# Eleven runs of products on zeros between the warm-up and the first real product

## The chip, the cores and the metric

One core of a Trainium2 chip runs the whole program. The metric is the device time of one execution in microseconds (us). Three runs of the kernel before took 2436.01, 2436.24 and 2447.96 us; the median is 2436.24.

## The reference

The reference runs a residual stream of 512 tokens by 1024 channels (float32) through two blocks. The first block has two layers. Each layer mixes a sliding-window attention, a short convolution and a diagonal complex recurrence (SSM) under gates, and then applies a gated feed-forward. The second block has a mixer with two kinds of sparse attention, a cross-attention to a memory of 256 rows, and a feed-forward with squared ReLU. Cut to what matters here, the beginning of the first layer:

```python
h = rmsnorm(x, norm_mix[i])
proj = h @ w_in[i]
q, k, v, cb, cc, cx, u, g = jnp.split(proj, IN_SPLITS, axis=-1)
...
lam_bar = jnp.exp(lam * dt)          # tables of the recurrence, from the inputs alone
_, states = lax.associative_scan(combine, (a_elems, bu), axis=1)
```

## The kernel before

Channels lie on the 128 partitions and the 512 tokens along the free axis. A value is kept as the sum of two float32r parts, high and low, and a product of weights and values is three float32r passes (lines 437 to 439): high by high, high by low, low by high. Weights come in 373 chunks of 128 by 1024 float32, each with eight 128 by 128 blocks. A chunk is loaded by SP's queue into one of three raw buffers, split by ScalarE (line 369, high part) and VectorE (line 370, low part) into one of three split buffers, and used by TensorE. Loads and splits are emitted with a raised priority.

The program is written as one sequence with side work (generators that are advanced between chunks). A scheduler then orders the instructions of each engine by priority, which is mostly program order, and by when its own model thinks that their inputs are ready; it also sets the waits. So an engine's order can differ from the program's: an instruction far down may come first where the engine would have nothing else to do.

The start goes so. SP loads a part of the vectors, the eight input tiles X, the first weight chunks and the constants (lines 1992 to 2001). GpSimd fills a bf16 tile `wz` with zeros (line 2008), and TensorE runs 16 warm-up products on it into one PSUM bank (line 2011), whose result is never read. Then the first norm splits each X[m] (lines 457 and 461) and adds up squares (lines 535 to 539, some of the additions on GpSimd). VectorE begins the tables of the recurrence (`_ssm_tables`, lines 818 to 1000), which need vectors only. `_gen_mix` computes the first result `u` of four tiles from 96 products in k-major order, with the norm's sums (line 492) and its broadcast (line 503) between the chunks, and evacuates it (line 579) with the row factor of the norm. After it come k, v and q.

PSUM has four banks for products under the tag `mm`, which go round; `u` holds all four. SBUF tiles under the same tag share their place: `wz` has the tag of the table `ssmc` (loaded at lines 960 and 961), and the tables `Wr` and `Wi` (lines 974 to 979) have the tags `wr` and `wi`. `Wr` and `Wi` have one column filled first (lines 976 and 977) and then copies and products written into them.

Of the kernel before, what the change touches and what calls it, by code (L numbers as in the profile page):

```python
# [11 lines left out]
FT = mybir.dt.float32  # L12
FR = mybir.dt.float32r
# [5 lines left out]
PSUM = bass.MemoryType.PSUM  # L19
DRAM = bass.MemoryType.DRAM  # L20
# [13 lines left out]
# ---------------------------------------------------------------- host layout  # L34
# [67 lines left out]
def _constants():  # L102
    """Arrays that depend on shapes alone."""
    f = np.float32
    lay = _cst_layout()
    c = np.zeros((128, lay["_n"][0]), f)

    def put(name, a):
        s, n = lay[name]
        c[:, s:s + n] = a  # L110
    put("ident", np.eye(128, dtype=f))
    q = np.arange(128)[:, None]
    j = np.arange(128)[None, :]
    put("mask1", np.concatenate([np.where(j > q, 0.0, NEG), np.where(j <= q, 0.0, NEG)], 1))
    t = np.arange(512).reshape(4, 128).T
    end = np.arange(32) * 16 + 31
    mc = np.where((end[None, None, :] <= t[:, :, None]) & (np.arange(32) < 31), 0.0, NEG)
    put("maskc", mc.reshape(128, 128))
    put("valid", (t >= 31).astype(f))
    put("stack", (np.arange(128)[:, None] % 32 == np.arange(128)[None, :] % 32).astype(f))  # L120
    put("ones2", 1.0)
    put("half2", (np.arange(128)[:, None] // 64 == np.arange(2)[None, :]).astype(f))
    rope = np.zeros((4, 128, 512), f)
    pos = np.arange(512, dtype=f)
    inv = (f(500000.0) ** (-np.arange(0, 16, 2, dtype=f) / f(16))).astype(f)
    ang = pos[:, None] * inv[None, :]
    cos, sin = np.cos(ang).T, np.sin(ang).T
    rope[0] = 1.0
    for h in (0, 64):
        rope[0, h:h + 8] = cos  # L130
        rope[0, h + 8:h + 16] = cos
        rope[1, h:h + 8] = -sin
        rope[1, h + 8:h + 16] = sin
    inv2 = (f(10000.0) ** (-np.arange(32, dtype=f) / f(32))).astype(f)
    ang = pos[:, None] * inv2[None, :]
    cos, sin = np.cos(ang).T, np.sin(ang).T
    C = np.concatenate([cos[:16], cos[:16], cos[16:], cos[16:]])
    S = np.concatenate([-sin[:16], sin[:16], -sin[16:], sin[16:]])
    rope[2] = np.concatenate([C, C])
    rope[3] = np.concatenate([S, S])  # L140
    cc = np.zeros((128, 256), f)
    n = end[:31]
    cc[:31, :128] = rope[2][:, n].T
    cc[:31, 128:] = rope[3][:, n].T
    put("crope", cc)
    return c, rope


def _host_pack(x, ins):
    """Layout only: transposes, permutations, repeats and zero padding."""  # L150
# [122 lines left out]
# ---------------------------------------------------------------- device  # L273
class _Net:
# [26 lines left out]
    # ---- memory  # L301
# [5 lines left out]
    def rslot(self):  # L307
        """A slot whose every writer rounds to float32r."""
        s = self.free_r.popleft()
        self.low_r = min(self.low_r, len(self.free_r))  # L310
        return s
# [30 lines left out]
    # ---- weights  # L342
# [8 lines left out]
    def _dma_(self):  # L351
        i = self.wd
        t = self.wp.tile([128, 1024], FT, tag="raw", bufs=self.RAW, name="raw")
        # the first chunk in halves: the products can start on its front
        n = 512 if i == 0 else 1024
        for c in range(0, 1024, n):
            self.nc.sync.dma_start(t[:, c:c + n], self.T["wp"][i, :, c:c + n])
        self.raw[i] = t
        self.wd += 1
# [34 lines left out]
    # ---- scheduling  # L394
# [19 lines left out]
    # ---- products  # L414
    def prod(self, key, K, ms, rhs, evac, outer=True, kk=None, N=512):
        """out[m] = sum_k W[k,m].T @ rhs[k] in three float32r passes; yields after each chunk."""
# [35 lines left out]
    # ---- pieces  # L452
    def split(self, src, g=None):
        """src * g as the exact sum of two float32r parts."""
        nc = self.nc
        h, l = self.rslot(), self.rslot()
        nc.scalar.activation(h, src, AF.Copy, scale=1.0 if g is None else g)  # L457
        if g is None:
            nc.vector.tensor_tensor(l, src, h.bitcast(FT), op=OP.subtract)  # L459
        else:  # L460
            nc.vector.scalar_tensor_tensor(l, src, g, h.bitcast(FT), op0=OP.mult, op1=OP.subtract)
        return (h, l)
# [10 lines left out]
    def rsqrt(self, out, ps, n, scale, eps, p=128):  # L473
        """out = 1/sqrt(ps * scale + eps) on a few columns."""
# [14 lines left out]
    def few(self, out, lhs, rhs, start=True, stop=True):  # L489
        """out = lhs.T @ rhs with few columns: the rows of out in four column tiles side by side."""  # L490
        for c in range(0, 128, 32):
            self.nc.tensor.matmul(out[c:c + 32], lhs[:, c:c + 32], rhs, start=start, stop=stop,
                                  skip_group_check=True)

    def tok_sums(self, ps, src, nblk=4):
        """ps(blk) = sums of src over partitions, tokens on partitions."""
        for b in range(nblk):
            self.few(ps(b), src[:, b * 128:(b + 1) * 128], self.ones1)

    def bcast(self, r, out, psum, nblk=4, width=None):  # L500
        """out[c, tok] = r[tok] for all c."""
# [5 lines left out]
    def heads_back(self, src, t, dst):  # L507
        """dst = two float32r parts of channel tile t of src[n], tokens on partitions."""
# [6 lines left out]
    def parts(self, o, dst, n):  # L515
        """Query block n of four channel tiles, from one bank, as two float32r parts."""
# [7 lines left out]
    def apply_v(self, out, pt, v, start, stop):  # L524
        """out[q, d] += sum_k pt[k, q] v[k, d]; the queries in two column tiles."""
# [3 lines left out]
    # ---- norms: raw split first, the row factor is applied to the product  # L529
# [12 lines left out]
    def norm_fin(self, st):  # L542
        """side steps that turn the sums into st['rs'], the row factor on all partitions."""
# [16 lines left out]
def _gen_mix(N, i, X, st, st2, tab=None):  # L560
    """First block's mixing half of layer i."""
# [10 lines left out]
    # --- SSM input  # L572
# [18 lines left out]
    # --- q, k, v  # L591
# [32 lines left out]
    # --- conv  # L624
# [26 lines left out]
    # --- gated branches  # L651
# [39 lines left out]
    # --- SSM tail: gelu, glu  # L691
# [36 lines left out]
def _gen_attn1(N, i, qT, kv, out):  # L728
# [13 lines left out]
    def probs(n, P):  # L742
        """Probabilities of the eight heads of query block n over its two key blocks."""
# [74 lines left out]
def _ssm_tables(N, i):  # L818
    """exp, cos, sin of the discretised poles, and what follows from them, on few columns."""
# [87 lines left out]
    # (lam_bar - 1) / lam  # L907
# [22 lines left out]
    # powers of lam_bar  # L930
# [8 lines left out]
    # b_bar  # L939
# [24 lines left out]
    # rotation per chunk of 8 and decay per chunk  # L964
# [17 lines left out]
    while n < 64:  # L982
        # W^n, then W^(n..2n-1)
# [18 lines left out]
def _gen_ssm(N, i, Ud, Yd, Kd, out):  # L1002
    """Diagonal complex recurrence, 64 chunks of 8 steps; four rounds of 128 channels (8 groups)."""
# [11 lines left out]
    for r in range(4):  # L1015
        pr = slice(4 * r, 4 * r + 4)
        # inputs with (step, channel) on partitions, steps from last to first
# [28 lines left out]
        # state contribution of each chunk  # L1046
# [22 lines left out]
        # back to the fixed frame, moved on by one chunk  # L1069
# [13 lines left out]
        # output side: C lam^t, t = 0..7  # L1083
# [8 lines left out]
        # kernels inside a chunk  # L1092
# [88 lines left out]
def _gen_att2(N, X, st, st2, gg, mem=None):  # L1181
    """Second block's mixer. X gets the residual sum, st2 the next norm's pieces."""
# [14 lines left out]
    # ---- row factors of the two norms  # L1197
# [17 lines left out]
    # x waits in DRAM while the slots are short  # L1215
# [5 lines left out]
    def residual():  # L1221
        """The normed x that the block adds to."""
# [17 lines left out]
    def rope(src, g=None):  # L1240
        """Rotated src * g; src may be in PSUM."""
# [22 lines left out]
    # ---- latents, index keys, gates: the row factor s1 is folded into later ones  # L1264
# [10 lines left out]
    def latents():  # L1275
# [33 lines left out]
        # index keys: gain and bias after the rows are turned back, both halves alike  # L1309
# [3 lines left out]
        # index weights take the queries' row factor, which is positive  # L1313
# [13 lines left out]
    # ---- heads with a norm: the row factor goes into the softmax's scale  # L1327
# [13 lines left out]
    def fold(out, src, n, div, row, rowq, mul):  # L1341
        """out = mul * row / sqrt(src * row^2 / div + eps); src (b, head), one row factor for each b."""
# [46 lines left out]
    def values():  # L1389
        """Both value heads of two branches with the tokens on partitions."""  # L1390
# [20 lines left out]
    def latent_kv():  # L1411
        """The shared key and value head, tokens on partitions."""
# [29 lines left out]
    # ---- compressed keys and values  # L1442
# [23 lines left out]
    def compress(z, ws):  # L1466
# [21 lines left out]
        if z == 1:  # L1488
            # the values of a query head's group, on the diagonal blocks of the four heads' keys
# [35 lines left out]
    # ---- index scores and the choice of keys  # L1525
# [42 lines left out]
    # ---- attention: units (n, branch, t) of two heads, queries of block n over all keys up to it  # L1568
# [74 lines left out]
    def compressed():  # L1643
        """The branch over the compressed keys; all heads of a block at once."""
        for n in range(4):
# [20 lines left out]
            # rows before the first whole block see no key  # L1666
# [32 lines left out]
    # ---- the order of things  # L1699
# [79 lines left out]
def _gen_memkv(N, M):  # L1779
    """Keys and values of the memory; yields between the pieces."""  # L1780
# [52 lines left out]
    # norm of the row-scaled keys: eps meets the scaled mean square  # L1833
# [28 lines left out]
def _gen_mem2(N, X, st, st2, M):  # L1862
# [3 lines left out]
    # ---- queries  # L1866
# [115 lines left out]
def tile_two_blocks(ctx: ExitStack, tc: tile.TileContext, T, out, nch, parts=None, dump=None):  # L1982
# [23 lines left out]
    # the tensor engine's clock is up when the first data arrive  # L2006
# [3 lines left out]
    for _ in range(16):  # L2010
        nc.tensor.matmul(ps, wz[:, :128], wz, start=True, stop=True)
    st = N.new_norm()
# [9 lines left out]
    # gains of the norm between the blocks and of the next norm, in one  # L2022
# [90 lines left out]
```

## Time and profile before

| | before |
|---|---|
| median of three runs | 2436.24 us |
| span of the profiled execution | 2433.1 us |
| TensorE busy | 2398.7 us |
| VectorE busy | 1440.4 us |
| ScalarE busy | 858.6 us |
| first warm-up product | 1.31 us |
| first real product | 7.00 us |

The page of the profile gives the profiled execution's time as its span, from the first instruction to the last; the median of the runs is 3.1 us above it. A busy time of TensorE counts a tail after each product, so two products in a row overlap; what a product costs in a stream is the step between two starts. The granted clock (PEclk) is a share of 2.4 GHz.

### The profile page before, as it was taken

The numbers are of one execution on the slowest core, as the hardware profiler recorded it, in microseconds if no ns is written. First come the engines' busy times: TensorE is split into PE (matmuls) and PEld (weight loads), VectorE is DVE, ScalarE is ACT, GpSimd is POOL, SyncE is SP. The second block draws the span as 40 slices with busy tenths as digits, with TensorE's granted clock in tenths as the row PEclk, the third lists the DMA queues.
The fourth block names the chain that finished last, engine by engine and source line by source line (L and its number), as shares of the span: only waits on it lengthen the run. The fifth ranks groups of instructions, "written<-read, shape, count | busy, mean of one in ns | idle before, by whom it ended". The sixth has DMA issues, their size and how long they took to land. (4 is left out here: it accounts for less than half of the span.)

```text
span 2433.1 us, 33742 instructions
## 1 busy us (share of the span) xinstructions
PE 2398.7 (99%) x13354; PEld 1880.1 (77%) x13357; DVE 1440.4 (59%) x2894; ACT 858.6 (35%) x1442; POOL 28.7 (1%) x48
## 2 busy tenths in 40 slices
PE   8999999999999999999999999999899999999999
PEld 6777888888888877778888888887666677888887
DVE  9976567543434677755554343467979766543443
ACT  3233333422222323433333222243456545422321
POOL 1000000000000000000000000000000000000000
PEclk9999999999999999999999999999979999999999
DMA  5322332222222233233222223242201111222222
GB/s 189 100 87 91 113 100 95 91 92 95 104 95 96 104 108 93 83 100 102 95 94 89 95 95 104 96 145 82 96 2 58 49 70 54 94 95 96 95 94 80
DMA packets 96781, 225.98 MB, mean 93 GB/s; under 512 B 35440, under 2 KB 39664, under 8 KB 96624
## 3 DMA queue, kind: packets, MB, share of 16 engines
q1 hardware_dynamic: 96624, 223.84, 27.1%
q8 instruction: 105, 1.72, 0.3%
q14 instruction: 52, 0.43, 0.1%
HBM read 214.88 MB, written 8.91 MB: 92 GB/s over the span
## 5 line engine op out<-in xcount | busy, mean ns | idle before, releaser
L437 PE MATMUL mm<-r,hi 128*128 128x512 f32 x2928 | 1163.7, 398 | 3.1 <-DVE f L579 2.2
L439 PE MATMUL mm<-r,lo 128*128 128x512 f32 x2928 | 1157.2, 395 | 4.5 <-DVE lo L370 4.5
L438 PE MATMUL mm<-r,hi 128*128 128x512 f32 x2928 | 1157.2, 395 | 0.0
L369 ACT ACTIVATE hi<-raw 128x1024 fp32r<-128x1024 f32 (+1 forms) x374 | 395.3, 1057 | 1240.3 <-PE mm L438 857.2
L437 PEld LDWEIGHTS mm<-r,hi 128*128 128x128 f32 x2928 | 551.3, 188 | 145.2 <-issue 4.2
L439 PEld LDWEIGHTS mm<-r,lo 128*128 128x128 f32 x2928 | 551.1, 188 | 135.8 <-DVE lo L370 4.9
L438 PEld LDWEIGHTS mm<-r,hi 128*128 128x128 f32 x2928 | 551.4, 188 | 127.7
L370 DVE TENSOR_TENSOR lo<-raw,hi 128x1024 fp32r<-128x1024 f32 (+1 forms) x374 | 456.1, 1220 | 222.1 <-ACT hi L369 220.6
L1152 DVE TENSOR_TENSOR f<-mm,f 128x512 f32<-128x512 f32 x88 | 60.9, 692 | 235.0 <-PE mm L439 235.0
L663 DVE TENSOR_TENSOR f<-mm,f 128x512 f32<-128x512 f32 x48 | 33.1, 689 | 103.1 <-PE mm L439 99.4
L457 ACT ACTIVATE r<-f 128x512 fp32r<-128x512 f32 x108 | 68.2, 632 | 60.5 <-DVE f L1158 29.2
L459 DVE TENSOR_TENSOR r<-f,r 128x512 fp32r<-128x512 f32 x108 | 74.0, 688 | 10.6 <-ACT r L457 7.4
L1174 DVE TENSOR_TENSOR f<-mm,f 128x512 f32<-128x512 f32 x48 | 33.1, 690 | 65.5 <-PE mm L439 65.3
L1959 DVE SCALAR_TENSOR_TENSOR f<-mm,f 128x512 f32<-128x512 f32 x32 | 22.1, 692 | 81.1 <-PE mm L439 81.1
L1974 DVE TENSOR_TENSOR f<-mm,f 128x512 f32<-128x512 f32 x32 | 22.1, 692 | 64.8 <-PE mm L439 64.7
L1580 PE MATMUL sc<-f,f 64*128 64x128 f32 (+3 forms) x192 | 53.5, 510 | 0.5 <-DVE f L1654 0.3
L1616 DVE TENSOR_REDUCE sm<-sc 128x1 f32<-128x128 f32 (+3 forms) x96 | 43.9, 483 | 16.1 <-PE sc L1582 15.8
L1590 PE MATMUL pt<-cst,f 128*128 128x128 f32 x240 | 43.9, 294 | 6.3 <-ACT f L1622 5.4
L527 PE MATMUL ot<-f,f 128*64 128x64 f32 x960 | 46.6, 235 | 0.0
L457 ACT ACTIVATE r<-f,vec 128x512 fp32r<-128x512 f32 x48 | 34.3, 714 | 32.5 <-DVE f L1174 7.8
L527 PEld LDWEIGHTS ot<-f,f 128*64 128x64 f32 x960 | 36.5, 142 | 11.7 <-issue 9.8
L1622 ACT ACTIVATE f<-sc,sm,rqn 128x128 f32<-128x128 f32 (+3 forms) x64 | 38.9, 613 | 15.3 <-DVE sm L1617 15.3
(387 smaller groups left out, 1741.7 us busy)
## 6 DMA issues: line engine op xcount, KB each, us to landing
raw<-in_wp_dram SPq DMA_DIRECT2D x372, 512.0 KB, 3.5
f<-in_xT_dram SPq DMA_DIRECT2D x8, 256.0 KB, 4.7
ud<-f SPq DMA_DIRECT2D x8, 256.0 KB, 2.3
f<-ud SPq DMA_DIRECT2D x64, 32.0 KB, 3.4
f<-ud SPq DMA_DIRECT2D x8, 256.0 KB, 3.6
yd<-f SPq DMA_DIRECT2D x64, 32.0 KB, 2.1
f<-yd SPq DMA_DIRECT2D x8, 256.0 KB, 3.6
xd<-f SPq DMA_DIRECT2D x8, 256.0 KB, 2.2
```

The source lines that it names most:

```text
L369: self.nc.scalar.activation(h[:, s], r[:, s], AF.Copy)
L370: self.nc.vector.tensor_tensor(lo[:, s], r[:, s], h.bitcast(FT)[:, s], op=OP.subtract)
L437: nc.tensor.matmul(p, wh, rh, start=first, stop=False)
L438: nc.tensor.matmul(p, wh, rl, start=False, stop=False)
L439: nc.tensor.matmul(p, wl, rh, start=False, stop=last)
L457: nc.scalar.activation(h, src, AF.Copy, scale=1.0 if g is None else g)
L459: nc.vector.tensor_tensor(l, src, h.bitcast(FT), op=OP.subtract)
L527: self.nc.tensor.matmul(out[c:c + 64], pt[:, c:c + 64], v, start=start, stop=stop, skip_group_check=True)
L1152: V.tensor_tensor(z, ps, RS, op=OP.mult)
L1580: PE.matmul(ps[h][:, :w], q[t][hs, n * 128:(n + 1) * 128], k_of[br][hs, :w], start=True, stop=False)
L1590: PE.transpose(pt[:, b * 128:(b + 1) * 128], p[:, b * 128:(b + 1) * 128], N.ident)
L1616: V.tensor_reduce(f[:, h:h + 1], ps[h][:, :w], axis=AX.X, op=OP.max, negate=True)
```

## The change

Behind the 16 warm-up products, two tiles of 128 by 1024 are filled with zeros on GpSimd: `zr` in float32r under the tag `wr`, and `zf` in float32 under the tag `wi`. A second PSUM bank is taken from `mm`. Then 86 products are issued in eleven runs, all with `start` and `stop`, into one or two banks that nobody reads:

```diff
     for _ in range(16):
         nc.tensor.matmul(ps, wz[:, :128], wz, start=True, stop=True)
+    zr = N.keep([128, 1024], FR, "zr", "wr")
+    zf = N.keep([128, 1024], FT, "zf", "wi")
+    nc.gpsimd.memset(zr.bitcast(FT), 0.0)
+    nc.gpsimd.memset(zf, 0.0)
+    mm = nc.tensor.matmul
+    p2 = N.mm("warm2")
+    for k in range(8):
+        mm(ps, zr[:, :128], zr[:, 512:], start=True, stop=True)
+    for k in range(8):
+        mm((ps, p2)[k % 2], zr[:, (k % 4) * 128:(k % 4) * 128 + 128], zr[:, 512:], start=True, stop=True)
+    for k in range(8):
+        mm(ps[:, :384], zr[:, :128], zr[:, 512:896], start=True, stop=True)
+    for k in range(8):
+        mm(ps[:, :256], zr[:, :128], zr[:, 512:768], start=True, stop=True)
+    for k in range(8):
+        mm(ps[:, :128], zr[:, :128], zr[:, 512:640], start=True, stop=True)
+    for k in range(8):
+        mm(ps, zr[:, :128], zr[:, None, 512:768].to_broadcast([128, 2, 256]), start=True, stop=True)
+    for k in range(8):
+        mm((ps, p2)[k % 2], zr[64 * (k % 2):64 * (k % 2) + 64, :128], zr[64 * (k % 2):64 * (k % 2) + 64, 512:],
+           start=True, stop=True)
+    for k in range(8):
+        mm(ps, zr[:64, :128], zr[:64, 512:], start=True, stop=True)
+    for k in range(6):
+        mm(ps, zf[:, :128], zf[:, 512:], start=True, stop=True)
+    for k in range(8):
+        mm((ps, p2)[k % 2], zf[64 * (k % 2):64 * (k % 2) + 64, :128], zf[64 * (k % 2):64 * (k % 2) + 64, 512:],
+           start=True, stop=True)
+    for k in range(8):
+        mm(ps, wz[:, :128], wz, start=True, stop=True)
     st = N.new_norm()
```

The runs are numbered 1 to 11 in this order: 1 and 2 are float32r with 512 columns, 3 to 5 with 384, 256 and 128 columns, 6 reads 256 columns twice, 7 alternates between the two halves of the rows, 8 uses the upper half alone, 9 is float32 (six products), 10 is float32 on alternating halves, and 11 is bf16 as in the warm-up. Everywhere else the diff takes out comments and docstrings only.

## Rows read from the trace of the kernel before

**Rows 1.** The page: busy time of each engine, and the granted clock in 40 slices
```profile
PE 2398.7 (99%) x13354; PEld 1880.1 (77%) x13357; DVE 1440.4 (59%) x2894; ACT 858.6 (35%) x1442; POOL 28.7 (1%) x48
...
PEclk9999999999999999999999999999979999999999
```

**Rows 2.** Two stretches: length, busy time by engine, PEclk, DMA share, GB/s
```profile
core 0: us, PE busy (x) PEld busy (x) DVE busy (x) ACT busy (x) POOL busy (x), PEclk, DMA share, GB/s
7.00:40.04 33.04, 25.75 (x132) 19.64 (x132) 32.28 (x131) 15.14 (x22) 8.97 (x6) 0.95 0.60 216
17.50:22.00 4.50, 4.18 (x11) 3.29 (x12) 4.50 (x20) 0.00 (x0) 0.00 (x0) 0.63 0.66 227
```

**Rows 3.** Timeline of the start: start, length, engine, line, what, [idle before]
```profile
1.19 0.98 POOL L954 MEMSET bbz<- 128x512 f32 x2
...
1.31 5.42 PE L2011 MATMUL warm<-warm 128*128 128x512 bf16 x16 [1.31 <-POOL warm L2008]
...
5.06 1.18 PEld L2011 LDWEIGHTS <-warm 128*128 128x128 bf16 x6 [0.20 <-issue]
...
7.00 0.50 PE L437 MATMUL mm<-r,hi 128*128 128x512 f32 x1 [0.27 <-ACT hi L369]
```

**Rows 4.** Timeline of TensorE: the products behind its waits up to 100 us
```profile
17.82 0.50 PE L439 MATMUL mm<-r,lo 128*128 128x512 f32 x1 [4.48 <-DVE lo L370]
...
30.15 0.43 PE L492 MATMUL nsum<-cst,f 128*32 128x1 f32 x32 [0.50 <-DVE f L847]
...
40.04 0.50 PE L437 MATMUL mm<-r,hi 128*128 128x512 f32 x1 [2.22 <-DVE f L579]
...
98.56 0.66 PE L1099 MATMUL k<-f,bbz 128*32 128x128 f32 x14 [0.46 <-DVE f L1090]
```

**Rows 5.** Timeline of VectorE and SP: the tables and the first evacuation
```profile
0.82 0.07 DVE L976 MEMSET wr<- 128x16 f32 x1 [0.82 <-PEq L2101]
...
28.30 0.36 SPq L960 DMA_DIRECT2D ssmc<-in_sc_dram  x1
...
38.85 0.18 DVE L978 COPY wr<-f 128x16 f32<-128x16 f32 x1
38.93 1.06 DVE L579 TENSOR_TENSOR f<-mm,f 128x512 f32<-128x512 f32 x1
```

**Rows 6.** Timeline of TensorE: float32r products in a row, 512, 256 and 128 columns
```profile
1887.09 0.39 PE L1853 MATMUL xv<-hi,r 128*128 128x512 f32 x1
...
1893.15 0.40 PE L1852 MATMUL xv<-hi,r 128*128 128x512 f32 x1
...
1880.55 0.28 PE L438 MATMUL mm<-r,hi 128*128 128x256 f32 x1
...
1883.16 0.28 PE L439 MATMUL mm<-r,lo 128*128 128x256 f32 x1
...
1710.62 0.27 PE L1420 MATMUL uk<-lo,r 128*128 128x128 f32 x1
...
1711.29 0.27 PE L1420 MATMUL uk<-lo,r 128*128 128x128 f32 x1
```

**Rows 7.** TensorE, plain float32: one line's records, then the timeline
```profile
L1902 PE MATMUL xs<-mk,f x32: 379/382/795, 2022.7 to 2041.9; 128*128 128x256 f32 x32
...
2022.69 2.06 PE L1902 MATMUL xs<-mk,f 128*128 128x256 f32 x8
2024.69 0.84 PE L492 MATMUL qs<-cst,f 128*32 128x1 f32 x64
...
2034.18 0.60 PE L1902 MATMUL xs<-mk,f 128*128 128x256 f32 x2
2034.62 0.38 PE L1907 MATMUL pt<-cst,f 128*128 128x128 f32 x2
...
1935.77 1.13 PE L1580 MATMUL sc<-f,f 64*128 64x512 f32 x4
1936.84 0.60 PE L1582 MATMUL sc<-bias,identb 128*128 128x512 bf16 x2
```

## The prediction

> **What bounds the kernel now.** I read the page's busy times first: TensorE is busy for 2398.7 of 2433.1 us and its granted clock is near full in almost every slice [rows 1], so anything put into TensorE's stream costs its own length unless it falls into a hole of that stream. Then the start of the timeline [rows 3]: the 16 warm-up products start at 1.31 us and end at 6.73, and the first real product starts at 7.00, when ScalarE has split the first weights. The reader should see that TensorE has no hole here: the dummies begin where the warm-up ends, and the first real product moves back by nearly their whole length. Third, the holes a little later [rows 4]: after a few products TensorE waits 4.48 us until 17.82 for VectorE's split of a weight chunk (line 370), 0.50 us before the norm's sums at 30.15, 2.22 us before 40.04 for VectorE's evacuation of the first result (line 579), and 0.46 us at 98.56. In between the clock falls: granted 0.63 in 17.5 to 22, which is partly the lower of the two levels, 1.2 GHz, right after the 4.48 us pause [rows 2]. VectorE is busy for 32.28 of the 33.04 us from 7.00 to 40.04 [rows 2], so these holes are VectorE being late; work that TensorE gets later gives VectorE time.
>
> The span of the profiled execution is 2433.1 us, and the median of the runs is 2436.24; I add differences in the span to the median, which lies 3.1 us above.
>
> **The change part by part.** Nothing is removed. Two fills of 1024 float32 columns on GpSimd, and 86 products in eleven runs on TensorE, are added; their result is never read.
>
> *The fills.* Two fills of 512 float32 columns took 0.98 us [rows 3], so the two new ones take about 2 us behind the warm-up's own fill, and are done near 3.2 us, under the warm-up products that last to 6.73. Cost nothing. Queued behind them on GpSimd are the fills of bbz, whose data VectorE only copies near 37 us, and the norm's additions, which wait for ScalarE until after 8 us. Were the cover gone, it would be those 2 us.
>
> *The products.* The price of one is the step from its start to the next start, not its busy time, which includes a tail. Runs 1, 2, 6 and 8 are 32 float32r products of 512 columns: first and last of 27 such products are 1887.09 and 1893.15 us, 26 steps of 0.233 us [rows 6]; 32 x 0.233 = 7.46. (Run 8 has half of the rows and the same columns; no row shows it alone, so it takes the same price.) Run 4, 256 columns: 22 steps from 1880.55 to 1883.16, 0.119 each [rows 6], 8 make 0.95. Run 5, 128 columns: 6 steps from 1710.62 to 1711.29, 0.112 each, as if something other than the columns set it; 8 make 0.89. Run 3, 384 columns, has no row: between 0.119 and 0.233, so 0.95 to 1.86; I take the middle, 1.41. Run 11, bf16: the warm-up's last six weight loads lie in 1.18 us with 0.15 for the last one, about 0.206 a step [rows 3], 8 make 1.65.
>
> Plain float32 is dearer. The 16 products of line 1902 leave 32 records [rows 7]: each is two instructions. One product of 256 columns takes 0.44 us until the next instruction (2034.18 to 2034.62), and four in a row take 2.00 (2022.69 to 2024.69), 0.50 each. At 512 columns that is 0.88 to 1.0; six products of run 9 make 5.28 to 6.0, I take 5.28.
>
> Runs 7 and 10 alternate between the upper and lower 64 rows, and between two banks. Line 1580 does this: two float32 products of 512 columns on the two halves (four records) go from 1935.77 to 1936.84, 1.07 us for both, where one on all rows would cost 0.88 [rows 7]. So the halves run side by side, with 0.2 us on top. Run 10, four such pairs: 4 x 1.07 = 4.28; without the 0.2 it would be 3.5, and one after the other 7.0. Run 7, four float32r pairs: 0.93 side by side, 1.86 in sequence, I take 0.93 + 0.2 = 1.13.
>
> A page of the Trainium skill, TensorEngine Tiling (Array Packing), section Tiling Modes, says that a change of the tiling mode makes TensorE drain. The 0.2 us after a pair [rows 7] agree with that; by the rule they are paid once when run 10 ends and not between its pairs, run 10 is 4 x 0.88 + 0.2 = 3.7, and the time comes out 0.6 us below my forecast.
>
> Sum: 7.46 + 1.41 + 0.95 + 0.89 + 1.13 + 5.28 + 4.28 + 1.65 = 23.05 us. From both ends it is 21.5 (0.95 for run 3, 0.93 for 7, 5.2 for 9, 3.5 for 10) to 27.7 (1.86, 1.86, 6.0, 7.0). The dummies start about 6.5, so the first real product starts at 29.5 instead of 7.00, 22.5 us later.
>
> *What is caught up.* By 29.5 us three weight chunks (as many buffers as there are) and the normed inputs can be ready, because VectorE and ScalarE need nothing from TensorE for them. The 96 products of the first result then run without a pause: 96 x 0.233 = 22.4, plus 0.43 for the norm's sums and about as much for its broadcast, 23.3 us. Before, the same stretch from 7.00 to 40.04 took 33.04 [rows 3, 4]. So up to 9.7 us come back: the three waits, their drained tails, and the time at the lower clock. The wait at 98.56 adds 0.5: up to 10.2. Next late is the evacuation of the first result: line 579 takes 1.06 us or more [rows 5] and may stand behind other work of VectorE, so I leave 0.6 of it and take 9.6. Nothing more can come back there: of all the waits, these are the ones on VectorE up to 100 us. Beyond that, TensorE's stream is shifted as a whole.
>
> *Waits that are added.* The zeros lie in the buffers that wr and wi get later, so VectorE's fill of wr, at 0.82 us before [rows 5], now waits for run 8 (about 18 us), and that of wi for run 10 (about 28). The first other writer of wr comes at 38.85 [rows 5], so there is cover if VectorE's order has the fills late. The load of ssmc, issued at 28.30 [rows 5], waits for run 11, 29.5: some 1.2 us in which SP holds two rope tables and the next weight chunk behind it; with three chunks in hand no one waits.
>
> Net: 22.5 - 9.6 = 12.9 us; 2436.24 + 12.9 = 2449.2 us.
>
> **The rivals.**
> - *No slower that one can tell (within 0.5%, 12.2 us).* The pairs of halves stream without the 0.2 us between them, the 384-column run goes at 256-column price, and the first evacuation is in time: block 21.5, later by 21.0, all 10.2 caught up, 10.8 us, 2447.0. For it: VectorE gains 22 us of time, and pairs do overlap. Against it: no row shows pairs in a row. It decides from a block of 21.9 us on, if all is caught up.
> - *The halves don't overlap in a long run.* Run 7 1.86 and run 10 7.0: 3.5 more, 2452.7. For it: each pair in the trace is followed by other work, so a second pair behind a first was never seen.
> - *VectorE is held by the fills of wr and wi.* At 0.82 they stood ahead of everything [rows 5]. If they keep a place soon after the first chunk's split, near 8.4 us, VectorE stands still to 28, 19.6 us, and the chain to line 579 (38.93) ends that much later: nothing is caught up, because TensorE now waits at the evacuation to about 59.6 where 52.9 would do. Net about 19.5, 2455.8. Against it: they are late in the program, and went first only because VectorE had nothing else at 0.82.
> - *The dummies are dropped, or the order of the later stages moves.* The result is unread, so a compiler could leave them out (2436.2); against it, the warm-up products are unread too and all 16 are in the trace [rows 3]. A shifted order of the attention stages could give or take some 3 us, rarely more.
>
> **How the numbers follow.** Forecast 0.40 (its own range 2448.4 to 2451.5), not told apart 0.28, halves in sequence 0.14, VectorE held 0.12, dropped or a luckier order 0.06. A measurement of this kernel tells about 0.5% from no change, 12.2 us, and the forecast is only just beyond that: slower 0.40 + 0.14 + 0.12 = 0.66, of which I give 0.03 to the edge, so 0.63; same 0.28 + 0.03 + 0.02 = 0.33; faster 0.04. The range runs from 2444 (the low block, and 3 us for the order) to 2460 (block at 27.7, half of the catch-up, 2458.4, and some scatter: one of the three runs shown lies 11.7 us above the others).
>
> **What would show it.** The first real product at 28 to 31 us; float32 dummies 0.88 apart, pairs in runs 7 and 10 at the price of one; full granted clock from there past 22 us of products; no wait on line 370, and under 1 us on line 579; the fill of wr late in VectorE's order. Wrong if the first real product starts before 27 or after 34, if real products stand between dummies, or if TensorE's later waits differ from before by more than 3 us.

## The result, and the profile after

The changed kernel takes 2455.73 us (median of four runs: 2455.03, 2455.72, 2455.74 and 2462.46), the kernel before 2436.43 (median of four as well). The ratio is 1.0073, with a 95% interval of 1.0048 to 1.0099: 19.3 us slower, where 12.9 were forecast (2449.2, range 2444 to 2460). The direction and the range held. The execution that was profiled is the slowest of the four; a second profile of the same program, experiment e10 below, shows an execution of 2455 us.

The page of after (the same parts as [rows 1]):

```profile
PE 2425.8 (99%) x13457; PEld 1896.1 (77%) x13457; DVE 1447.2 (59%) x2894; ACT 858.6 (35%) x1442; POOL 29.9 (1%) x50
...
PEclk8999999999999999999999999999979999999999
```

TensorE is busy for 27.1 us more. That is more than the 22.5 us of the dummies; part of the rest is that a product counts as busy for longer where the clock is low (0.63 us at 54.32 below, 0.40 at 58.01). The first slice of the granted clock has become worse (8 after 9): the clock falls somewhere in the first 61 us, although TensorE now has no pause between 7 and 41 us.

Stretches of after, with the columns of [rows 2]:

```profile
7.00:30.00 23.00, 23.00 (x104) 14.60 (x103) 23.00 (x95) 10.50 (x18) 8.29 (x6) 1.00 0.64 233
30.00:41.40 11.40, 11.40 (x80) 8.99 (x79) 10.96 (x52) 1.06 (x1) 0.00 (x0) 1.00 0.08 24
41.40:53.00 11.60, 0.42 (x3) 0.02 (x1) 10.91 (x57) 1.06 (x1) 0.00 (x0) 0.62 0.15 45
53.00:58.00 5.00, 5.00 (x14) 4.09 (x15) 4.26 (x6) 0.60 (x1) 0.53 (x1) 0.52 0.15 36
58.00:70.00 12.00, 12.00 (x53) 9.67 (x52) 6.25 (x6) 2.12 (x2) 1.05 (x2) 1.00 0.39 139
```

Here is the answer to [rows 2]: from 7 to 41.4 us TensorE is never idle, and the clock is full. Then, from 41.4 to 53, TensorE does nothing (0.42 us) while VectorE is busy for 10.91 of 11.60 us. In the 5 us behind that the clock is 0.52, nearly all of it the lower level of 1.2 GHz. So TensorE now waits once and long, on an engine that has no idle time to give.

The timeline of TensorE in after (start, length, engine, line, what, [idle before]), which answers to [rows 3, 4]:

```profile
1.31 6.22 PE L2011 MATMUL warm<-warm 128*128 128x512 bf16 x16 [1.31 <-POOL warm L2008]
7.18 2.19 PE L2020 MATMUL warm<-zr 128*128 128x512 f32 x8
9.21 1.98 PE L2022 MATMUL warm<-zr 128*128 128x512 f32 x8
11.02 1.57 PE L2024 MATMUL warm<-zr 128*128 128x384 f32 x8
12.44 1.11 PE L2026 MATMUL warm<-zr 128*128 128x256 f32 x8
13.38 1.01 PE L2028 MATMUL warm<-zr 128*128 128x128 f32 x8
14.23 2.07 PE L2030 MATMUL warm<-zr 128*128 128x512 f32 x8
16.23 1.19 PE L2032 MATMUL warm<-zr 64*128 64x512 f32 x8
17.26 1.98 PE L2035 MATMUL warm<-zr 64*128 64x512 f32 x8
19.17 5.42 PE L2037 MATMUL warm<-zf 128*128 128x512 f32 x12
24.52 3.70 PE L2039 MATMUL warm<-zf 64*128 64x512 f32 x16
28.16 1.90 PE L2042 MATMUL warm<-warm 128*128 128x512 bf16 x8
29.70 0.58 PE L437 MATMUL mm<-r,hi 128*128 128x512 f32 x1
...
35.58 0.43 PE L492 MATMUL nsum<-cst,f 128*32 128x1 f32 x32
...
41.41 0.40 PE L439 MATMUL mm<-r,lo 128*128 128x512 f32 x1
52.98 1.11 PE L503 MATMUL nb<-cst,rs 128*128 128x128 f32 x4 [11.18 <-DVE rs L487]
53.75 0.78 PE L437 MATMUL mm<-r,hi 128*128 128x512 f32 x1
54.32 0.63 PE L438 MATMUL mm<-r,hi 128*128 128x512 f32 x1
...
57.73 0.44 PE L437 MATMUL mm<-r,hi 128*128 128x512 f32 x1
58.01 0.40 PE L438 MATMUL mm<-r,hi 128*128 128x512 f32 x1
...
66.88 0.40 PE L437 MATMUL mm<-r,hi 128*128 128x512 f32 x1
```

The steps between the starts are the runs' prices: 2.03, 1.81, 1.42, 0.94, 0.85, 2.00, 1.03, 1.91, 5.35, 3.64 and 1.54 us, together 22.5. The first real product starts at 29.70, 22.7 us later than before. The waits of [rows 4] on lines 370 and 579 are gone. In their place TensorE waits 11.18 us for `rs`, the row factor of the norm, at the broadcast (line 503), which now stands behind 48 of the 96 products (counted in the trace; before it stood behind 90). The eight products from 54.32 to 57.73 are 0.426 us apart instead of 0.233, 1.5 us more. The second result starts at 66.88, 26.8 us later than the 40.04 of before: nothing was caught up, and 4.1 us were lost on top.

What VectorE did, in after's timeline:

```profile
34.53 0.07 DVE L976 MEMSET wr<- 128x16 f32 x1
...
38.95 0.07 DVE L977 MEMSET wi<- 128x16 f32 x1
...
47.37 0.41 DVE L923 TENSOR_TENSOR f<-wr 128x240 f32<-128x240 f32 x1
...
48.01 0.15 DVE L481 TENSOR_SCALAR ra<-nsum 128x4 f32<-128x4 f32 x1
...
52.18 0.68 DVE L923 TENSOR_TENSOR f<-wr 128x496 f32<-128x496 f32 x1
52.77 0.15 DVE L487 SCALAR_TENSOR_TENSOR rs<-rt,ry 128x4 f32<-128x4 f32 x1
```

The sums of the norm are done on TensorE at 36.0 us (35.58 + 0.43), but VectorE takes up the factor's chain (line 481) only at 48.01, because the tables of the recurrence (lines 923 to 928) stand ahead of it. In the kernel before, the same view has line 481 at 31.08 and `rs` at 35.57:

```profile
31.08 0.14 DVE L481 TENSOR_SCALAR ra<-nsum 128x4 f32<-128x4 f32 x1
...
35.57 0.14 DVE L487 SCALAR_TENSOR_TENSOR rs<-rt,ry 128x4 f32<-128x4 f32 x1
```

Among VectorE's instructions in the traces line 481 is number 114 before and number 202 after: 88 more stand ahead of it. (The expectations below give its place as 86 before and 170, 168, 106 and 122 in after, e2, e5 and e6; the traces have 202, 199, 137 and 153 for these. The differences are close to the same, 84 there and 88 here.)

### The profile page after: what moved, and what is told of

It is laid out like the page before. It is cut to its first block, busy times and chain, and to the rows that moved or that the text cites. A ratio compares the mean times of both kernels' runs of the same rounds, so it can differ in the third digit from the quotient of the medians.

```text
span 2460.7 us, 33949 instructions
## 1 busy us (share of the span) xinstructions
PE 2425.8 (99%) x13457; PEld 1896.1 (77%) x13457; DVE 1447.2 (59%) x2894; ACT 858.6 (35%) x1442; POOL 29.9 (1%) x50
## 5 line engine op out<-in xcount | busy, mean ns | idle before, releaser
L459 DVE TENSOR_TENSOR r<-f,r 128x512 fp32r<-128x512 f32 x108 | 74.1, 689 | 10.2 <-ACT r L457 6.9
```

## The experiments

Theory A: the order that the scheduler wrote for VectorE and TensorE makes the new wait, not a buffer that is still in use. Theory B was that the wait belongs to the one execution profiled, C that the buffers of the zeros hold VectorE, D that moving the tables only moves the cost, E that the time added is the block's length less the holes of before. "Later" below is always against the profile of the kernel before, at the start of the same weight split (line 369); for the second result it is the ninth, at 45.71 us before and 72.44 in after, 26.7 later.

**e1 and e10, the changed kernel again** (no edit).

> The changed kernel once more. Theory A (order): VectorE's fixed order has the norm factor's chain (lines 481 to 487) behind 84 more of the tables' instructions than before, so TensorE waits some 11 us before the broadcast (line 503) in every execution; first real product at 29.5 to 30, time 2455 to 2456 us. Theory B (chance): the 11 us belong to the one execution profiled, which was 6.7 us longer than the three others; then the wait is under 5 us here.

> The changed kernel once more, on the same chip. Theory A: first real product near 29 us, wait at the broadcast 11 to 13 us, second result 26 to 28 us later than in the profile of the kernel before. No rival differs here; it says how far two profiles of the changed kernel agree, and in which stretch they don't.

e1: 2462.88 us, ratio 1.0123 (1.0100 to 1.0145), 7 us above the 2455 to 2456 that was expected; e10: 2455.32 us, ratio 1.0083 (1.0043 to 1.0124). The wait at the broadcast is 12.58 us in e1 and 12.12 in e10, so B falls. TensorE in e10:

```profile
6.25 2.19 PE L2020 MATMUL warm<-zr 128*128 128x512 f32 x8
...
28.77 0.58 PE L437 MATMUL mm<-r,hi 128*128 128x512 f32 x1
...
52.99 1.12 PE L503 MATMUL nb<-cst,rs 128*128 128x128 f32 x4 [12.12 <-DVE rs L487]
```

The warm-up was 0.9 us shorter here than in after, and the broadcast came at the same time (52.99 and 52.98): the wait took up the difference (12.12 and 11.18). So the moment is set by VectorE alone, as A says. The spans of the two profiles differ by 7.4 us. At the second result it is 0.9 (26.7 later in after, 25.9 in e10), because behind the wait nine products run at the lower clock in after and four in e10. Most of the rest comes in the attention of the second block, where the clock falls for longer in one execution than in another. A stretch of it, the same work, first in before, then in after, then in e10 (columns of [rows 2]):

```profile
1780.00:1810.00 30.00, 29.46 (x337) 18.48 (x335) 22.64 (x82) 17.29 (x61) 0.00 (x0) 0.77 0.01 2
```

```profile
1805.00:1835.00 30.00, 29.54 (x330) 18.61 (x326) 22.25 (x81) 16.29 (x57) 0.00 (x0) 0.77 0.01 2
```

```profile
1805.00:1835.00 30.00, 28.53 (x372) 18.59 (x371) 26.34 (x96) 20.87 (x73) 0.00 (x0) 1.00 0.01 2
```

Over the whole attention (1745 to 1890 us in before) e10 wins back 4.5 us against before and after loses 0.8; another 1.2 us are lost in after, and none in e10, between 2000 and 2050. e1 goes as after does: 0.9 and 1.3. These are executions of one program, so these stretches say nothing about the change, and differences of a few us in a whole time can't be put down to an edit without the view of the place.

**e2, the same length in another shape.** Instead of the eleven runs, bf16 products on `wz`; the zeros are still filled and never read.

```diff
...
+    for k in range(106):
+        mm((ps, p2)[k % 2], wz[:, :128], wz, start=True, stop=True)
```

> The eleven runs are replaced by 106 bf16 products on the warm-up's own zeros, 106 x 0.215 = 22.8 us, as long as the runs were; both zero tiles stay but TensorE never reads them, so VectorE's fills of wr and wi wait for nothing of it. Theory A (order, set by how late the real products come): the chain of the norm factor stands at place 168 of VectorE's order against 170 after the change, so TensorE waits 9 to 12 us before the broadcast again and the time is 2454 to 2457 us. Theory C (the shared tags wr and wi hold VectorE): no wait, about 13 us less, 2442 to 2444 us.

2459.57 us, ratio 1.0102 (1.0085 to 1.0119), above the 2454 to 2457 that A expected and far from C's 2442 to 2444; the second result is 24.5 us later. The waits of TensorE up to 250 us (us in total, times, longest):

```profile
PE nb L503 <- DVE rs L487: 9.9, 1, 9.9
PE warm L2011 <- POOL warm L2008: 1.3, 1, 1.3
```

Neither `wr` nor `wi` is held by a product here, and the wait is the same in kind. C falls. After's own trace agrees: its fills of `wr` and `wi` run at 34.53 and 38.95 us without idle time before them. What the dummies compute makes little difference (24.5 us at the second result against 25.9 to 27.2 in the three profiles of the changed kernel).

**e9, the broadcast later in TensorE's order.** VectorE's order stays; the first broadcast is ordered behind 72 products.

```diff
+            yield
...
+                self.tc.add_manual_dep(t.ins, self.last_mm.ins.name, mybir.DependencyInfo(
+                    mybir.DependencyClass.NoSync, mybir.DependencyReason.DATA), reason="behind the third chunk")
```

> The changed kernel with the broadcast of the row factor (line 503) ordered behind 72 of the 96 products of the first result instead of 48; VectorE's order is untouched. Theory A (VectorE's order sets when the factor is ready, and TensorE's order sets how much of that is a wait): the factor is still ready near 52.8 us, TensorE now comes to the broadcast at about 41.4 + 24 x 0.233 = 47.0, the wait falls from 11.2 to about 6 us, and the second result starts about 5 us earlier than in the changed kernel (7 if the clock does not fall behind the shorter wait). Rival (the evacuation behind the broadcast sets the pace, so that it only moves the wait): the wait at the broadcast falls all the same, but as much comes back as a wait before the second result (line 579), and the time is that of the changed kernel.

```profile
53.01 1.11 PE L560 MATMUL nb<-cst,rs 128*128 128x128 f32 x4 [6.12 <-DVE rs L488]
```

TensorE in e9: the factor comes when it came, the wait is 6.12 us, and no wait on the evacuation follows. The second result is 20.7 us later, 5.2 less than in e10, as A had it; the rival falls. The whole time, 2454.11 us (ratio 1.0096, 1.0063 to 1.0129), is not told apart from e10's: the attention gave back 1.7 us in e9's profile and 4.5 in e10's.

**e3, the factor ahead of the tables.** In the changed kernel each operation of VectorE for the first layer's tables and recurrence that is written behind the norm's factor is ordered behind it as well. Nothing else is edited, and no semaphore is added.

```diff
+            r = f(*a, **k)
+            d = self._n.rs_ins
+            if d is not None:
+                self._n.tc.add_manual_dep(r.ins, d.ins.name, mybir.DependencyInfo(
+                    mybir.DependencyClass.NoSync, mybir.DependencyReason.DATA), reason="behind the row factor")
...
-    V = nc.vector
+    V = _Late(N, nc.vector) if i == 0 else nc.vector
```

> The changed kernel, with one order added on VectorE (no semaphore): the tables' instructions behind the first part, and the recurrence's first ones, stand behind the last instruction of the norm factor. Theory A: the wait of 11 us before the broadcast goes, the products of the first result run without a pause, and the clock does not fall; 11.2 + 1.7 us come back, 2442 to 2444 us, that is 6 to 8 us above the kernel before. Theory D (VectorE simply has too much work in the first 60 us): the tables are late now and hold TensorE elsewhere, below 110 us; the time stays at 2452 us or more.

2451.81 us, ratio 1.0068 (1.0053 to 1.0083). VectorE in e3 (line 481 is 501 here, 487 is 507 and 503 is 524), and then TensorE:

```profile
35.80 0.16 DVE L501 TENSOR_SCALAR ra<-nsum 128x4 f32<-128x4 f32 x1 [7.92 <-PE nsum L513]
...
38.99 0.16 DVE L507 SCALAR_TENSOR_TENSOR rs<-rt,ry 128x4 f32<-128x4 f32 x1
```

```profile
35.30 0.43 PE L513 MATMUL nsum<-cst,f 128*32 128x1 f32 x32
...
41.36 0.60 PE L524 MATMUL nb<-cst,rs 128*128 128x128 f32 x4
```

The factor is ready at 39.2 us, before TensorE comes to the broadcast, and no wait is left there. The second result is 13.2 us later, against 26.7 in after and 25.9 in e10: the order alone is worth 12.7 to 13.5 us at that point. The forecast for the whole change, 22.5 less 9.6, was 12.9. The time itself missed its expectation (2442 to 2444) and lies at the edge of D's (2452 or more). I had taken 13 us off the 2455.7 of the first runs; beside e1, which ran on the same chip, e3 is 11.1 us faster. D's reason is not there: up to 250 us TensorE's longest wait behind the start is 0.7 us. Later on, e3 falls back a little: 15.3 us later at 237 us and 16.9 at the end, while e10 goes from 25.9 to 20.2. So what the order is worth in the whole time, 11.1 us beside e1 and 3.5 beside e10, is not fixed by these runs.

**e4 and e7, the same edge in the kernel before.** e4 orders all tables behind the factor, those that come earlier in the program too (it takes out their early start); e7 has e3's edge.

```diff
-        with tc.high_priority(offset=-600):
-            next(tab)
```

> The kernel before, without any dummy run, with all of the tables' work on VectorE ordered behind the norm factor. If the holes of the start come from VectorE doing tables first (theory A's other half), the waits of 4.48 and 2.22 us and the time at the lower clock go, the second result starts at 31 to 33 us instead of 40.04, and the time is 2427 to 2430 us. Theory D: the tables are missing later and TensorE waits for them below 150 us, nothing is won: 2434 to 2440 us.

> The kernel before, without dummies, with the tables behind their first part ordered behind the norm factor on VectorE. Theory A: the wait of 4.48 us at 17.8 stays (the first part still stands ahead of the second chunk's split), the wait of 2.22 us at 40.04 goes or shrinks, so the second result starts 2 to 3 us earlier; later order changes take 2 to 4 us back, as in the changed kernel with the same edge. 2433 to 2438 us, not told apart from before.

e4: 2445.01 us, ratio 1.0057 (1.0035 to 1.0078). e7: 2441.46 us, ratio 1.0033 (1.0015 to 1.0051). Both are slower than any expectation for them. TensorE's waits up to 250 us, e4 and then e7 (L284 is the helper that records the ordered table operations):

```profile
PE k L1123 <- DVE at L783: 5.8, 1, 5.8
PE nsum L513 <- DMA cst<-in_cst_dram: 2.9, 1, 2.9
PE bl L1063 <- DVE f L284: 2.4, 1, 2.4
```

```profile
PE mm L457 <- DVE f L284: 6.1, 1, 6.1
PE mm L459 <- DVE lo L390: 4.5, 1, 4.5
```

e4's second result is 4.3 us earlier than before's; by 162 us it is 7.7 later, because the recurrence (line 1123) now waits for what was pushed back. D holds in the kernel before. In e7 the wait of 4.5 us on the weight split stays, and the pushed tables meet the evacuation instead, which starts at 42.98 us where before it started at 38.93: 6.1 us of wait ahead of the second result, 5.5 later in all, where I expected a gain. In e3 VectorE stood idle for 7.92 us just ahead of the factor, so there was room; in e7 it stood idle for 0.56 us there.

**e5, e6 and e8, parts of the change.** e5 keeps runs 9 and 10 alone, e6 all but these, e8 the fills alone.

```diff
-    for k in range(6):
-        mm(ps, zf[:, :128], zf[:, 512:], start=True, stop=True)
-    for k in range(8):
-        mm((ps, p2)[k % 2], zf[64 * (k % 2):64 * (k % 2) + 64, :128], zf[64 * (k % 2):64 * (k % 2) + 64, 512:],
-           start=True, stop=True)
```

(This is e6's; e5 and e8 take out the other runs, and all.)

> Only the two plain float32 runs (9 and 10, 9.0 us in the changed kernel) and the two fills. Theory A (order): the first real product at about 16, but the norm factor's chain stands at place 106 of VectorE's order (86 before, 170 after the change) and the broadcast now behind 48 of the 96 products instead of 90; the factor is ready at 38 to 39, TensorE waits about 11 us before the broadcast from about 27.5, and the second result starts some 12 us later than before: a block of 9 us costs more than its length, 2445 to 2449 us. Theory E (length of the block less the holes it fills): 9.0 us vanish in the holes of some 10 us, 2434 to 2438 us.

> Without the two plain float32 runs: runs 1 to 8 and 11, 13.7 us in the changed kernel. Theory A: first real product at 20.5 to 21, the chain at place 122, the factor ready near 42.6, a wait of 8 to 10 us before the broadcast, the second result 14 to 16 us later than before: 2448 to 2453 us. Theory E: 13.7 less some 10, 2438 to 2441 us.

> The two fills on GpSimd and the two tiles under the tags wr and wi, and none of the 86 products. All theories but C: the fills lie under the warm-up, nothing changes, 2433 to 2437 us. Theory C (tags): VectorE's fills of wr and wi now wait for GpSimd's fills, to 3.2 us at most, and VectorE's start is later by up to 2 us.

| | first real product | line 481 in VectorE's order | second result later | time | ratio |
|---|---|---|---|---|---|
| before | 7.00 | 114 | 0 | 2436.4 | 1 |
| e8 | 7.02 | 113 | 0.7 | 2439.02 | 1.0022 (1.0006 to 1.0038) |
| e5 | 15.73 | 137 | 9.7 | 2443.06 | 1.0036 (1.0020 to 1.0051) |
| e6 | 20.33 | 153 | 15.0 | 2452.69 | 1.0068 (1.0047 to 1.0089) |
| e10 | 28.77 | 202 | 25.9 | 2455.32 | 1.0083 (1.0043 to 1.0124) |
| e3 | 29.42 | 89 | 13.2 | 2451.81 | 1.0068 (1.0053 to 1.0083) |

Each ratio is against the kernel before on the same chip (2435.2 to 2436.0 us). Waits of TensorE up to 250 us in e5, then in e6:

```profile
PE nsum L492 <- DVE f L539: 6.6, 1, 6.6
```

```profile
PE nb L503 <- DVE f L1067: 5.2, 1, 5.2
PE nsum L492 <- DVE f L539: 2.3, 1, 2.3
```

The longer the dummies last, the further back the scheduler puts line 481; the norm's sums come earlier among the products in all three (behind 24, 69 before). That its model held TensorE to be late, and so filled VectorE with tables, fits these places, but no run shows it. E falls: 8.9 us of dummies (6.85 to 15.73) cost 9.7 us at the second result and not next to nothing. A was roughly right on the cost of e5 (some 12 us expected at the second result, and 2445 to 2449 us in all) and wrong on the place, the wait of 11 us before the broadcast: 6.6 us lie before the sums, which wait for the last addition of squares (line 539) near 28 us, and only 0.5 before the broadcast. In e6 the expected 14 to 16 us were measured as 15.0; the wait before the broadcast, 5.2 us, is shorter than the expected 8 to 10. The fills cost 0.7 us at the second result in e8, and its median, 2439.02 us, is 2 us above what was expected. The profile of e8 is 2.6 us later up to 1900 us and 16 at the end. Nearly all of that is lost in one stretch, in e8 and then in before:

```profile
1907.00:1937.00 30.00, 30.00 (x136) 16.97 (x137) 13.60 (x35) 11.37 (x38) 0.00 (x0) 0.50 0.01 3
```

```profile
1904.00:1922.00 18.00, 17.71 (x138) 10.67 (x137) 13.45 (x38) 11.43 (x38) 0.00 (x0) 1.00 0.04 16
```

It is the same work, at the lower clock in e8 although TensorE is busy through all of it, and for 9.30 of the 10 us ahead of it in both: 2.6 us late at its start and 15.1 at its end. The profile of e6, the slowest of its four executions (2458.61, the fastest 2448.47), loses 12.4 us in the same place, after's and e10's nothing. So e6's and e8's times hold executions with this loss, and the table's times are less good a measure of the change than its second results.

## Why the prediction was right or wrong, point by point

- *Bound by TensorE, no hole at the dummies' place:* right. They run from 7.18 without a gap.
- *The price of the block:* right, 22.5 us against 23.05. The float32r runs 1, 2, 6 and 8 took 7.75 against 7.46, run 3 1.42 against 1.41, run 9 5.35 against 5.28. Run 10 took 3.64 against 4.28: its pairs are 0.91 us apart, where the pair of [rows 7] took 1.07 with other work behind it. Here the rule of the Trainium skill, TensorEngine Tiling (Array Packing), section Tiling Modes, that TensorE drains when the mode changes, agrees with the trace in that no 0.2 us stand between the pairs: its 3.7 for run 10 was nearer than my 4.28.
- *First real product at 29.5:* 29.70 (28.77 in e10).
- *The fills cost nothing:* nearly; 0.7 us at the second result of e8.
- *The old waits go:* right for lines 370 and 579. *Full clock from there:* right up to 41.4 us, wrong behind the new wait.
- *What is caught up, 9.6 of at most 10.2 us:* this step failed. It was -4.1 us in after: 22.7 later at the first product of the first result, 26.8 at that of the second. In e10 the two are 21.8 and 26.0. The working says that VectorE and ScalarE "need nothing from TensorE" for the weight chunks and the normed inputs, and that held. For the norm's factor it has no term at all: the broadcast enters with its own 0.43 us, as if the factor were ready when TensorE wants it. But the factor needs the norm's sums from TensorE, and VectorE's place for it was fixed when the program was scheduled. I moved TensorE's stream by 22.5 us and left the orders of the engines as they were in the trace before. They were written anew: the factor went behind 88 more operations, the broadcast from behind 90 products to behind 48. That gives the wait of 11.2 us and the low clock behind it. e3 repairs the order alone, and its second result is 13.2 us later where 12.9 had been worked out.
- *The range held by luck.* 25.9 to 27.2 us were lost by the second result in after, e1 and e10, some 1.1 came back in the stages of k up to 155 us, and the execution profiled in e10 took 4.5 back in the second block's attention, by a clock that differs between executions. e1, four more runs of the same program, took 2462.88 us, outside the range. The forecast's 12.9 and the measured 19.3 are closer together than the mechanisms are.
- *Rivals.* Not told apart: refuted, the block was 22.5 and nothing caught up. (Its limit was worked out wrongly: 12.2 and 10.2 us are 22.4 us of delay, which is a block of 22.9 us, not 21.9, when the dummies start at 6.5.) The halves in sequence: refuted by runs 7 and 10. VectorE held by the fills of `wr` and `wi`: its 19.5 us met the result, but its mechanism is refuted by e2 and by the fills at 34.53 and 38.95; the sister that was true (VectorE's order, with no buffer in it) was not on the list beyond a remark on "a luckier order". Dropped: refuted.
- *Wrong if the later waits differ by more than 3 us:* they do, by the 11.2 us, and by its own test the prediction's account was wrong there.

What stays open: why the clock falls in the attention of one execution and not in that of another, by which the profiles of 2455 us (e10) and of 2462 (after and e1) differ most, and why the scheduler chose the places that it chose.

## What to carry to other kernels

Here work added to one engine reached another through the order that the scheduler wrote for it. A trace of the kernel before gives the length of an addition and not where the rest will stand; before the gaps are counted as cover, list each chain that goes from the lengthened engine to another and back, and ask what may be put in front of it. When the result is in, look for a new wait on an engine that was busy all through it, compare the two orders of that engine, and repair the one order before believing any other cause. Time won at one point is only won if a later view, hundreds of microseconds on, still shows it.

## What the runs showed of the hardware

- Pairs of products on the two halves of the rows run side by side, four pairs in a row: four float32 pairs in 3.64 us, 0.91 a pair, against 0.89 for one float32 product on all rows (5.35 over six). Four float32r pairs took 1.03 us, 0.26 each against 0.23.
- Half of the rows saves nothing without its partner: eight products on 64 rows took 1.91 us, eight on 128 rows 1.81 to 2.03.
- How long the clock stayed low behind the wait did not follow the wait's length: six products at the lower clock behind a pause of 6.12 us (e9), four behind 12.12 (e10), nine behind 11.18 (after) and ten behind 12.58 (e1), the same program in the last three. Their starts are 0.426 us apart, against 0.233 at full clock.
- The clock can be at the lower level for 30 us while TensorE is busy all the time, and only in some executions: granted 0.50 from 1907 to 1937 us in e8's profile, 1.00 for the same work in before's, with 9.30 of the 10 us ahead of it busy in both. It cost e8 12.5 us.
